# Alternating emission of two heads' scores and two quarters' state space inputs, with the causal masks behind the scores

## The chip, the cores and the metric

The kernel runs on one core of a Trainium2 chip. The metric is the time of one execution on the device in microseconds. Three runs of the kernel before stand beside one profiled execution, which has a time of its own.

## The reference, cut to what matters

Four transformer layers over 256 tokens with a width of 1024 follow each other. The change lies in the third one, whose mixer has two halves: a stick-breaking attention of eight heads of 64, and a state space model of 32 groups with 64 complex states each.

```python
def stick_breaking_attention(q, k, v):            # per block of 128 queries
    z = jnp.einsum('bqhd,bshd->bhqs', q_b, k) * scale
    causal = (spos[None, :] < tpos[:, None])[None, None]
    log_beta = jax.nn.log_sigmoid(z)
    log_1mb = jnp.where(causal, jax.nn.log_sigmoid(-z), 0.0)
    csum = jnp.cumsum(log_1mb, axis=-1)
    log_w = log_beta + csum[..., -1:] - csum
    w = jnp.where(causal, jnp.exp(log_w), 0.0)
    return jnp.einsum('bhqs,bshd->bqhd', w, v)

def s5_ssm(u, ...):
    bu_r = jnp.einsum('bsgc,gnc->bsgn', uf, bbar_r)     # the inputs
    bu_i = jnp.einsum('bsgc,gnc->bsgn', uf, bbar_i)
    x = lax.associative_scan(...)                       # x[s] = a x[s-1] + bu[s]
    return (jnp.einsum('gcn,bsgn->bsgc', c_re, x_r)     # the outputs
            - jnp.einsum('gcn,bsgn->bsgc', c_im, x_i) + d * uf)

def mixer_sb_ssm(x, ...):
    a_out = stick_breaking_attention(q, k, v)
    y = gelu(s5_ssm(u, ...))
    y = y * sigmoid(y @ w_glu + b_glu)
    return concatenate([a_out, y]) @ w_out
```

## The kernel before

All weights are read from HBM in the order of one list and split into a high part (ScalarE, L363) and a low part (VectorE, some on GpSimd, L366). A large product is then three matmuls with full 128 rows: high by high, high by low, low by high (`mm3`, L388 to L390). These products run all the time; they are called the stream here. In the third layer's mixer, while the stream computes keys, queries and values (the names sk, sq, sv in the list), two generators stand at the side and are advanced one step at each `yield` of the stream: `side_attention` and `_ssm_run`. The instructions that they emit are then ordered by the scheduler that builds the program; each engine runs its own in that order, one behind the other. The order can be read from the built program.

`side_attention` goes over the eight heads. `stage_a` writes the scores of one head into one bank of PSUM: a causal mask by a matmul of the identity (L1324, 128 rows), then keys by queries, whose 64 dimensions lie in rows 0 to 63 or 64 to 127 (L1325, and L1327 for the second block of keys). ScalarE and VectorE make the softplus of it (L1330 to L1333). `stage_b` subtracts its sums with triangular matmuls in the same bank (L1338, L1340, L1342) and takes the exponential (L1345). `stage_c` multiplies two heads by the values (L1353). Banks come from a pool of four, called psw; a head holds its bank from the scores to the exponential.

`_ssm_run` takes the 16 pairs of groups in four sets (k) of four quarters (q). A quarter's input is two matmuls of 64 rows (L1887) into a bank; the quarter's number decides which half of the rows. VectorE rotates it (L1891, L1892), GpSimd combines (L1893, L1894), VectorE scans over the tokens (L1896, two scans a quarter), and VectorE and GpSimd rotate back (L1906 to L1913). `outputs` (L1851, L1856, L1859) multiplies the states by the output matrix for the set before, and VectorE adds the skip term (L1861). The scans of a set write a buffer that the outputs of an earlier set read. Behind the last set come the gelu (ScalarE and VectorE, L1659 to L1664), its high and low parts (L464, L465) and the gate's matmuls (`glu`), which the stream's next products need. [...]

Of the kernel before, what the change touches and what calls it, by code (L numbers as in the profile page):

```python
# [11 lines left out]
AF = mybir.ActivationFunctionType  # L12
ALU = mybir.AluOpType
# [482 lines left out]
class _Norm(_Act):  # L496
# [8 lines left out]
    def slice(self, xT, c):  # L505
        self.add(xT[:, 2 * c:2 * c + 2], self.g[:, 2 * c:2 * c + 2])
        if c == 0:
            self.e.after = self.last
        self.square(xT, c)
# [779 lines left out]
def _second(e, K, xT, act, S, ln, out, dump):  # L1289
    nc, tc = e.nc, e.tc  # L1290
    V, A, G, PE = nc.vector, nc.scalar, nc.gpsimd, nc.tensor
# [3 lines left out]
    D = {}  # L1295
# [4 lines left out]
    for c in range(2):  # L1300
        e.run(e.transposed(("su", c), act,
                           lambda b, bank, c=c: A.activation(out=uT[:, 2 * c:2 * c + 2], in_=bank, func=AF.Copy)))
# [13 lines left out]
    smask2 = im[:, 1].unsqueeze(1).to_broadcast([128, 2, 128])  # L1316
    sc, ws = {}, {}

    def stage_a(s):
        j, g = s // 2, s % 2  # L1320
        hs = slice(64 * g, 64 * g + 64)
        ps = e.bank()
        diag = ps[:, :].rearrange("p (a q) -> p a q", a=4)[:, 0:4:2]
        PE.matmul(out=diag, lhsT=im[:, 0], rhs=smask2, start=True, stop=False, skip_group_check=True)  # L1324
        PE.matmul(out=ps[:, 0:256], lhsT=kT[hs, j, 0:128], rhs=qT[hs, j, :], start=False, stop=False,  # L1325
                  skip_group_check=True)
        PE.matmul(out=ps[:, 256:384], lhsT=kT[hs, j, 128:256], rhs=qT[hs, j, 128:256], start=False, stop=False,  # L1327
                  skip_group_check=True)
        l = e.t("b2", [128, 384])
        A.activation(out=l, in_=ps[:, :384], func=AF.Abs)  # L1330
        A.activation(out=l, in_=l, func=AF.Exp, scale=-1.0)
        A.activation(out=l, in_=l, func=AF.Ln, bias=1.0)
        V.scalar_tensor_tensor(out=l, in0=ps[:, :384], scalar=0.0, in1=l, op0=ALU.max, op1=ALU.add)  # L1333
        sc[s] = (ps, l)

    def stage_b(s):
        ps, sp = sc.pop(s)
# [22 lines left out]
        D["done"] = j + 1  # L1360

    def side_attention():
        ready, lag = [], 1
        for s in range(8 + lag):
            while s >= 4 and "qk" not in D:
                yield
            if s < 8:
                stage_a(s)
            if s >= lag:
                stage_b(s - lag)  # L1370
                if (s - lag) % 2:
                    ready.append((s - lag) // 2)
            yield
            if ready and "v" in D:
                stage_c(ready.pop(0))
        while ready:
            yield
            stage_c(ready.pop(0))
# [464 lines left out]
def _ssm_run(e, P, C, S, uT, yT):  # L1843
# [32 lines left out]
    for k in range(4):  # L1876
        w = e.t("b4", [128, 4, 2, 128])
        xs = e.t("b4", [128, 4, 2, 128])
        s = slice(4 * k, 4 * k + 4)
        mt = e.t("b2", [128, 4, 128])  # L1880
        G.tensor_tensor(out=mt, in0=C["j01"].unsqueeze(1).to_broadcast([128, 4, 128]),
                        in1=S["m"][:, s].unsqueeze(2).to_broadcast([128, 4, 128]), op=ALU.mult)
        for q in range(4):
            h = slice(64 * (q % 2), 64 * (q % 2) + 64)
            ps = e.bank()[:, :256].rearrange("p (c j) -> p c j", c=2)
            for c in range(2):
                PE.matmul(out=ps[:, c], lhsT=S["bT"][h, c, 2 * k + q // 2], rhs=up[h, k, q // 2])  # L1887
            st = 4 * k + q
            tc_ = e.t("b1", [128, 2, 128])
            ts_ = e.t("b1", [128, 2, 128])  # L1890
            V.tensor_tensor(out=tc_, in0=ps, in1=S["cos"][:, st].unsqueeze(1).to_broadcast([128, 2, 128]), op=ALU.mult)  # L1891
            V.tensor_tensor(out=ts_, in0=ps, in1=S["sin"][:, st].unsqueeze(1).to_broadcast([128, 2, 128]), op=ALU.mult)  # L1892
            G.tensor_tensor(out=w[:, q, 0], in0=tc_[:, 0], in1=ts_[:, 1], op=ALU.add)  # L1893
            G.tensor_tensor(out=w[:, q, 1], in0=tc_[:, 1], in1=ts_[:, 0], op=ALU.subtract)  # L1894
            for c in range(2):
                V.tensor_tensor_scan(out=xs[:, q, c], data0=mt[:, q], data1=w[:, q, c], initial=0.0,  # L1896
                                     op0=ALU.mult, op1=ALU.add)
            if q % 2:
                yield
        if prev is not None:  # L1900
            outputs(*prev)
        cosb = S["cos"][:, s]
        sinb = S["sin"][:, s]
        ta = e.t("b2", [128, 4, 128])
        tb = e.t("b2", [128, 4, 128])
        V.tensor_tensor(out=ta, in0=xs[:, :, 0], in1=cosb, op=ALU.mult)  # L1906
        G.tensor_tensor(out=tb, in0=xs[:, :, 1], in1=sinb, op=ALU.mult)
        V.tensor_tensor(out=w[:, :, 0], in0=ta, in1=tb, op=ALU.subtract)
        tc2 = e.t("b2", [128, 4, 128])
        td = e.t("b2", [128, 4, 128])  # L1910
        V.tensor_tensor(out=tc2, in0=xs[:, :, 1], in1=cosb, op=ALU.mult)
        G.tensor_tensor(out=td, in0=xs[:, :, 0], in1=sinb, op=ALU.mult)
        V.tensor_tensor(out=w[:, :, 1], in0=tc2, in1=td, op=ALU.add)  # L1913
        prev = (k, w)
        yield
# [176 lines left out]
```

## Time and profile before

| what | value |
|---|---|
| three runs | 1475.64, 1476.12, 1477.32 us, median 1476.12 |
| profiled execution | 1473.14 us, its span 1471.4 us, mean granted clock of TensorE 0.993 |
| busy share of the span | TensorE 98%, VectorE 74%, ScalarE 53%, GpSimd 19% |
| the stretch of the change | about 896 to 967 us of the span |

The span reaches from the first to the last instruction in the trace. Busy shares are averages over stages with different limits. A matmul's record is longer than the time to the next one's start, since matmuls overlap; what a matmul takes of TensorE is read from start to start.

### The profile page before, as it was taken

How to read it: one execution, taken by the hardware profiler on the slowest of the kernel's cores; microseconds unless marked ns; L12 is line 12 of the kernel's file. 1: busy time of each engine (PE TensorE's matmuls, PEld its weight loads, DVE VectorE, ACT ScalarE, POOL GpSimd, SP SyncE). 2: the span in 40 equal slices, each digit the busy share in tenths (PEclk: the TensorE clock that was granted, in tenths of full speed). 3: DMA queues.
4: the chain of work that ended last, by engine and by line, in shares of the span. 5: the costliest groups of instructions: out<-in, count | busy, mean ns of one | idle time of the engine just before them, and what ended most of it. 6: DMA issues, size and time to landing. Idle time of an engine off the chain costs nothing.

```text
span 1471.4 us, 24711 instructions
## 1 busy us (share of the span) xinstructions
PE 1435.8 (98%) x9636; PEld 1269.1 (86%) x9636; DVE 1090.3 (74%) x1820; ACT 784.9 (53%) x1258; POOL 274.5 (19%) x201
## 2 busy tenths in 40 slices
PE   9999999999999999999999999999999998999997
PEld 6878999999998779999999998778888796788886
DVE  7796669666678696679877778877666688686666
ACT  6665545444556564455645555365444465654442
POOL 2343314000045343213000337510000100100000
PEclk9999999999999999999999999999999998999999
DMA  8553555655546653555565453336556362366551
GB/s 291 188 179 109 173 172 177 198 186 187 178 146 195 198 172 130 173 166 191 188 198 180 154 185 122 101 129 216 192 181 198 123 220 75 100 208 193 186 190 69
DMA packets 70677, 250.66 MB, mean 170 GB/s; under 512 B 8096, under 2 KB 8480, under 8 KB 70560
## 3 DMA queue, kind: packets, MB, share of 16 engines
q1 hardware_dynamic: 70560, 249.07, 51.6%
q8 instruction: 76, 1.25, 0.3%
q14 instruction: 41, 0.34, 0.1%
HBM read 247.99 MB, written 1.05 MB: 169 GB/s over the span
## 4 chain that ended last, share of the span: by engine, by line
PE 49%; DVE 4%; issue 1%; ACT 1%; POOL 0%; DVEq 0%; POOLq 0%
PE psw L438 11%; PE psa L388 9%; PE psa L390 9%; PE psa L389 9%; PE psw L440 6%; DVE lo L366 1%; DVE b L1896 1%; PE psw L2033 1%; PE psw L389 0%; PE psw L2019 0%; PE psw L390 0%; ACT b L1607 0%; PE psw L1887 0%; PE psw L388 0%; DVE b L1984 0%
## 5 line engine op out<-in xcount | busy, mean ns | idle before, releaser
L366 DVE TENSOR_TENSOR lo<-raw,hi 128x1024 fp32r<-128x1024 f32 (+1 forms) x409 | 512.5, 1260 | 216.7 <-ACT hi L363 215.9
L363 ACT ACTIVATE hi<-raw 128x1024 fp32r<-128x1024 f32 (+1 forms) x448 | 465.7, 1047 | 386.8 <-issue 141.4
L438 PE MATMUL psw<-act,hi 128*128 128x512 f32 x960 | 340.7, 397 | 0.0
L440 PE MATMUL psw<-act,lo 128*128 128x256 f32 x960 | 268.0, 281 | 0.0
L438 PEld LDWEIGHTS psw<-act,hi 128*128 128x128 f32 x960 | 179.9, 188 | 41.0
L440 PEld LDWEIGHTS psw<-act,lo 128*128 128x128 f32 x960 | 181.5, 189 | 1.7
L390 PE MATMUL psa<-b,lo 128*128 128x256 f32 x640 | 180.5, 283 | 0.0
L389 PE MATMUL psa<-b,hi 128*128 128x256 f32 x640 | 180.2, 283 | 0.0
L388 PE MATMUL psa<-b,hi 128*128 128x256 f32 x640 | 177.8, 283 | 0.0
L388 PE MATMUL psa<-act,hi 128*128 128x256 f32 x456 | 132.2, 291 | 0.0
L390 PE MATMUL psa<-act,lo 128*128 128x256 f32 x456 | 130.3, 286 | 0.5 <-DVE lo L366 0.5
L389 PE MATMUL psa<-act,hi 128*128 128x256 f32 x456 | 130.8, 287 | 0.0
L366 POOL TENSOR_TENSOR lo<-raw,hi 128x1024 fp32r<-128x1024 f32 x39 | 96.0, 2461 | 173.7 <-ACT hi L363 158.9
L389 PE MATMUL psa<-lo,act 128*128 128x512 f32 (+2 forms) x320 | 121.6, 383 | 3.6 <-DVE lo L366 2.6
L388 PE MATMUL psa<-hi,act 128*128 128x512 f32 (+2 forms) x320 | 122.3, 390 | 1.6 <-ACT hi L363 1.2
L390 PEld LDWEIGHTS psa<-b,lo 128*128 128x128 f32 x640 | 122.1, 191 | 0.1
L389 PEld LDWEIGHTS psa<-b,hi 128*128 128x128 f32 x640 | 122.0, 191 | 0.0
L388 PEld LDWEIGHTS psa<-b,hi 128*128 128x128 f32 x640 | 120.5, 191 | 1.2
L390 PE MATMUL psa<-hi,act 128*128 128x512 f32 (+2 forms) x320 | 117.9, 382 | 0.0
L388 PE MATMUL psa<-hi,b 128*128 128x512 f32 x256 | 99.7, 391 | 0.0
L389 PE MATMUL psa<-lo,b 128*128 128x512 f32 x256 | 99.6, 390 | 0.0
L390 PE MATMUL psa<-hi,b 128*128 128x512 f32 x256 | 98.7, 389 | 0.0
(360 smaller groups left out, 2692.2 us busy)
## 6 DMA issues: line engine op xcount, KB each, us to landing
raw<-in_ws_dram SPq DMA_DIRECT2D x450, 512.0 KB, 4.1
b<-in_ln_dram SPq DMA_DIRECT2D x8, 512.0 KB, 5.1
raw<-in_ws_dram SPq DMA_DIRECT2D x8, 280.0 KB, 3.7
raw<-in_ws_dram SPq DMA_DIRECT2D x4, 264.0 KB, 2.7
b<-in_x_dram SPq DMA_DIRECT2D x4, 256.0 KB, 5.0
out_dram<-b SPq DMA_DIRECT2D x4, 256.0 KB, 2.0
cb<-in_cb_dram SPq DMA_DIRECT2D x1, 676.0 KB, 7.1
b<-in_p_dram SPq DMA_DIRECT2D x2, 256.0 KB, 5.0
```

The costliest lines, as they stand in the source:

```text
L363: self.nc.scalar.activation(out=hi, in_=w, func=AF.Copy)
L366: eng.tensor_tensor(out=lo, in0=w, in1=hi.bitcast(F32), op=ALU.subtract)
L388: mm(out=out, lhsT=lh, rhs=rh, start=start, stop=False, skip_group_check=shared)
L389: mm(out=out, lhsT=lh, rhs=rl, start=False, stop=False, skip_group_check=shared)
L390: self.mlast = mm(out=out, lhsT=ll, rhs=rh, start=False, stop=stop, skip_group_check=shared)
L438: mm(out=bank.rearrange("p (v t) -> p v t", v=2), lhsT=h[:, c], rhs=act[2][k], start=k == 0, stop=False, skip_group_check=True)
L440: mm(out=bank[:, :256], lhsT=l[:, c], rhs=act[0][k], start=False, stop=k == len(hi) - 1, skip_group_check=True)
L1896: V.tensor_tensor_scan(out=xs[:, q, c], data0=mt[:, q], data1=w[:, q, c], initial=0.0, op0=ALU.mult, op1=ALU.add)
L2033: PE.matmul(out=o[64 * gg:64 * gg + 64, q0:256], lhsT=vw[:, kt, v0:v0 + 64], rhs=pts[s - 1 + gg][:, 256 * kt:256 * kt + 256 - q0], start=k ...
```

## The change

`stage_a` now handles a pair of heads j: it takes two banks, emits the first score matmul of both heads, then the second of both, and the two masks behind them. The softplus of both heads follows. `side_attention` goes over four pairs and runs `stage_b` of both heads a step later. In `_ssm_run` the inputs of two quarters are emitted together, alternating between the halves of the rows, into two banks. What is computed stays the same.

```diff
@@ -1316,22 +1316,26 @@
     smask2 = im[:, 1].unsqueeze(1).to_broadcast([128, 2, 128])
     sc, ws = {}, {}
 
-    def stage_a(s):
-        j, g = s // 2, s % 2
-        hs = slice(64 * g, 64 * g + 64)
-        ps = e.bank()
-        diag = ps[:, :].rearrange("p (a q) -> p a q", a=4)[:, 0:4:2]
-        PE.matmul(out=diag, lhsT=im[:, 0], rhs=smask2, start=True, stop=False, skip_group_check=True)
-        PE.matmul(out=ps[:, 0:256], lhsT=kT[hs, j, 0:128], rhs=qT[hs, j, :], start=False, stop=False,
-                  skip_group_check=True)
-        PE.matmul(out=ps[:, 256:384], lhsT=kT[hs, j, 128:256], rhs=qT[hs, j, 128:256], start=False, stop=False,
-                  skip_group_check=True)
-        l = e.t("b2", [128, 384])
-        A.activation(out=l, in_=ps[:, :384], func=AF.Abs)
-        A.activation(out=l, in_=l, func=AF.Exp, scale=-1.0)
-        A.activation(out=l, in_=l, func=AF.Ln, bias=1.0)
-        V.scalar_tensor_tensor(out=l, in0=ps[:, :384], scalar=0.0, in1=l, op0=ALU.max, op1=ALU.add)
-        sc[s] = (ps, l)
+    def stage_a(j):
+
+        pss = [e.bank() for _ in range(2)]
+        for o, n in ((0, 128), (256, 256)):
+            for g in range(2):
+                hs = slice(64 * g, 64 * g + 64)
+                PE.matmul(out=pss[g][:, o:o + 384 - n],
+                          lhsT=kT[hs, j, n - 128:n], rhs=qT[hs, j, n - 128:256], start=o == 0, stop=False,
+                          skip_group_check=True)
+        for g in range(2):
+            diag = pss[g].rearrange("p (a q) -> p a q", a=4)[:, 0:4:2]
+            PE.matmul(out=diag, lhsT=im[:, 0], rhs=smask2, start=False, stop=False, skip_group_check=True)
+        for g in range(2):
+            ps = pss[g]
+            l = e.t("b2", [128, 384])
+            A.activation(out=l, in_=ps[:, :384], func=AF.Abs)
+            A.activation(out=l, in_=l, func=AF.Exp, scale=-1.0)
+            A.activation(out=l, in_=l, func=AF.Ln, bias=1.0)
+            V.scalar_tensor_tensor(out=l, in0=ps[:, :384], scalar=0.0, in1=l, op0=ALU.max, op1=ALU.add)
+            sc[2 * j + g] = (ps, l)
 
     def stage_b(s):
         ps, sp = sc.pop(s)
@@ -1360,19 +1364,18 @@
         D["done"] = j + 1
 
     def side_attention():
-        ready, lag = [], 1
-        for s in range(8 + lag):
-            while s >= 4 and "qk" not in D:
+        ready = []
+        for j in range(4):
+            while j >= 2 and "qk" not in D:
                 yield
-            if s < 8:
-                stage_a(s)
-            if s >= lag:
-                stage_b(s - lag)
-                if (s - lag) % 2:
-                    ready.append((s - lag) // 2)
+            stage_a(j)
             yield
-            if ready and "v" in D:
-                stage_c(ready.pop(0))
+            for g in range(2):
+                stage_b(2 * j + g)
+                if ready and "v" in D:
+                    stage_c(ready.pop(0))
+            ready.append(j)
+            yield
         while ready:
             yield
             stage_c(ready.pop(0))
@@ -1881,10 +1884,13 @@
         G.tensor_tensor(out=mt, in0=C["j01"].unsqueeze(1).to_broadcast([128, 4, 128]),
                         in1=S["m"][:, s].unsqueeze(2).to_broadcast([128, 4, 128]), op=ALU.mult)
         for q in range(4):
-            h = slice(64 * (q % 2), 64 * (q % 2) + 64)
-            ps = e.bank()[:, :256].rearrange("p (c j) -> p c j", c=2)
-            for c in range(2):
-                PE.matmul(out=ps[:, c], lhsT=S["bT"][h, c, 2 * k + q // 2], rhs=up[h, k, q // 2])
+            if q % 2 == 0:
+                pss = [e.bank()[:, :256].rearrange("p (c j) -> p c j", c=2) for _ in range(2)]
+                for c in range(2):
+                    for n in range(2):
+                        h = slice(64 * n, 64 * n + 64)
+                        PE.matmul(out=pss[n][:, c], lhsT=S["bT"][h, c, 2 * k + q // 2], rhs=up[h, k, q // 2])
+            ps = pss[q % 2]
             st = 4 * k + q
             tc_ = e.t("b1", [128, 2, 128])
             ts_ = e.t("b1", [128, 2, 128])
```

Below, three places of the two orders. The line numbers of the changed kernel are a few higher: the scores are its L1325, the mask L1330, the last step of the softplus L1337, the triangular matmuls L1342, L1344 and L1346, the inputs of a quarter L1892, GpSimd's part L1899 and L1900, the scans L1902, the last rotation L1919 and the outputs L1854, L1859 and L1862. The order names a scan SCALAR_TENSOR_TENSOR.

TensorE, where the inputs of k = 1 begin, before (psw is a bank; the number behind it tells banks apart):

```order
L1887 MATMUL psw_10231<-b_1691_10035,b_1487_8648 128x128 x2
L1887 MATMUL psw_10242<-b_1691_10035,b_1487_8648 128x128 x2
L1324 MATMUL psw_10253<-b_1683_9995 128x2x128
L1325 MATMUL psw_10253<-b_1680_9992,b_1681_9993 128x256
L1327 MATMUL psw_10253<-b_1680_9992,b_1681_9993 128x128
```

and now:

```order
L1892 MATMUL psw_10231<-b_1691_10035,b_1487_8648 128x128
L1892 MATMUL psw_10232<-b_1691_10035,b_1487_8648 128x128
L1892 MATMUL psw_10231<-b_1691_10035,b_1487_8648 128x128
L1892 MATMUL psw_10232<-b_1691_10035,b_1487_8648 128x128
L1325 MATMUL psw_10253<-b_1680_9992,b_1681_9993 128x256
L1325 MATMUL psw_10254<-b_1680_9992,b_1681_9993 128x256
L1325 MATMUL psw_10253<-b_1680_9992,b_1681_9993 128x128
L1325 MATMUL psw_10254<-b_1680_9992,b_1681_9993 128x128
L1330 MATMUL psw_10253<-b_1683_9995 128x2x128
L1330 MATMUL psw_10254<-b_1683_9995 128x2x128
```

The two quarters alternate, head 1 (psw_10254) has come up from 24 stream matmuls farther down to stand beside head 0, and the masks are last. Heads 6 and 7 stand in the same way later; head 3 stands 14 stream matmuls behind head 2, head 5 nine behind head 4.

TensorE, at the outputs of k = 0 (psw_10365) and the triangular matmuls of heads 0 and 1 (psw_10253, psw_10254), now:

```order
L1854 MATMUL psw_10365<-b_1664_9866,b_1512_8803 128x128
L1859 MATMUL psw_10365<-b_1692_10069,b_1455_8452 32x128 x4
L1325 MATMUL psw_10394<-b_1680_9992,b_1681_9993 128x256
L1325 MATMUL psw_10394<-b_1680_9992,b_1681_9993 128x128
L1859 MATMUL psw_10365<-b_1692_10069,b_1455_8452 32x128 x4
L1862 MATMUL psw_10365<-b_1692_10069,b_1455_8452 32x127 x6
L1342 MATMUL psw_10253<-b_1736_10261,cb_7507 128x256
L1344 MATMUL psw_10253<-b_1736_10261,ones_64 128x128
L1346 MATMUL psw_10253<-b_1736_10261,cb_7507 128x128
L1342 MATMUL psw_10254<-b_1737_10266,cb_7507 128x256
```

Before, head 0's triangular matmuls stood in the middle of these outputs and head 1's behind them; both are now in one row near the end, behind the scores of head 2 (psw_10394). 26 stream matmuls stand between this place and the second set of quarters ahead of it, where there were 24.

VectorE at the same place, before (b_1735 and b_1743 are the softplus of heads 0 and 1):

```order
L1913 TENSOR_TENSOR b_1692_10069<-b_1716_10185,b_1717_10186 128x4x128
L1333 SCALAR_TENSOR_TENSOR b_1735_10257<-psw_10253,b_1735_10257 128x384
L1896 SCALAR_TENSOR_TENSOR b_1726_10228<-b_1727_10229,b_1725_10227 128x128 x4
L1333 SCALAR_TENSOR_TENSOR b_1743_10313<-psw_10309,b_1743_10313 128x384
L366 TENSOR_TENSOR lo_10475<-raw_10106,hi_10474 128x1024
```

and now:

```order
L1919 TENSOR_TENSOR b_1692_10069<-b_1716_10185,b_1717_10186 128x4x128
L1902 SCALAR_TENSOR_TENSOR b_1726_10228<-b_1727_10229,b_1725_10227 128x128 x4
L1337 SCALAR_TENSOR_TENSOR b_1736_10261<-psw_10253,b_1736_10261 128x384
L1902 SCALAR_TENSOR_TENSOR b_1726_10228<-b_1727_10229,b_1725_10227 128x128
L1337 SCALAR_TENSOR_TENSOR b_1737_10266<-psw_10254,b_1737_10266 128x384
L1902 SCALAR_TENSOR_TENSOR b_1726_10228<-b_1727_10229,b_1725_10227 128x128
L366 TENSOR_TENSOR lo_10480<-raw_10106,hi_10479 128x1024
```

Four scans that stood behind head 0's softplus stand ahead of it. On GpSimd L1893 and L1894 of one quarter have moved ahead of a weight split L366 there. The order of the DMA queue is unchanged. In the fourth layer's sparse attention, which the change doesn't touch, the scheduler has moved a few value products (L2033) and score matmuls past each other.

## Rows read from the trace of the kernel before

**Rows 1.** The page, busy us of an engine, share, instructions.

```profile
PE 1435.8 (98%) x9636; PEld 1269.1 (86%) x9636; DVE 1090.3 (74%) x1820; ACT 784.9 (53%) x1258; POOL 274.5 (19%) x201
```

**Rows 2.** Windows: stretch, length, busy PE, PEld, DVE, ACT, POOL, clock, DMA, GB/s.

```profile
912.00:919.00 7.00, 5.99 (x46) 5.26 (x45) 7.00 (x12) 3.52 (x7) 4.78 (x3) 1.00 0.25 77
```

**Rows 3.** Waits of PE from 896 to 968: us in total, times, longest.

```profile
PE psw L1338 <- DVE b L1333: 2.2, 3, 1.0
```

**Rows 4.** Timeline of DVE: scans of k = 2, and the way out.

```profile
928.54 4.72 DVE L1896 TENSOR_TENSOR_SCAN b<-b,b 128x128 f32<-128x128 f32 x8 [2.06 <-PE psw L1859]
...
952.71 0.68 DVE L1913 TENSOR_TENSOR b<-b,b 128x512 f32<-128x512 f32 x1
...
955.39 0.48 DVE L1861 SCALAR_TENSOR_TENSOR b<-b,prm,psw 128x256 f32<-128x256 f32 x1 [1.68 <-PE psw L1859]
...
964.30 1.23 DVE L465 TENSOR_TENSOR b<-b,b 128x1024 fp32r<-128x1024 f32 x1
```

**Rows 5.** Timeline of PE: outputs of k = 3, and the gate's first matmuls.

```profile
954.25 0.65 PE L1856 MATMUL psw<-b,b 128*32 128x128 f32 x16
...
966.96 0.39 PE L390 MATMUL psa<-hi,act 128*128 128x512 f32 x1
967.19 0.41 PE L388 MATMUL psw<-b,hi 128*128 128x256 f32 x2
```

**Rows 6.** Timeline of PE around one quarter: start, us, instruction.

```profile
886.01 0.71 PE L1887 MATMUL psw<-b,b 64*128 64x128 f32 x4
886.65 0.39 PE L388 MATMUL psa<-act,hi 128*128 128x256 f32 x1
```

**Rows 7.** Timeline of PE, two quarters and one head's scores.

```profile
900.71 0.28 PE L389 MATMUL psa<-act,hi 128*128 128x256 f32 x1
900.83 0.28 PE L390 MATMUL psa<-act,lo 128*128 128x256 f32 x1
901.04 0.72 PE L1887 MATMUL psw<-b,b 64*128 64x128 f32 x8
901.69 0.38 PE L1324 MATMUL psw<-b 128*128 128x256 f32 x1
902.00 0.70 PE L1325 MATMUL psw<-b,b 64*128 64x256 f32 x2
...
902.85 0.39 PE L388 MATMUL psa<-act,hi 128*128 128x256 f32 x1
```

**Rows 8.** Timeline of DVE at the outputs of k = 0.

```profile
905.39 0.86 DVE L1913 TENSOR_TENSOR b<-b,b 128x512 f32<-128x512 f32 x1
906.18 0.54 DVE L1333 SCALAR_TENSOR_TENSOR b<-psw,b 128x384 f32<-128x384 f32 x1
906.64 3.71 DVE L1896 TENSOR_TENSOR_SCAN b<-b,b 128x128 f32<-128x128 f32 x4
...
911.87 1.36 DVE L1896 TENSOR_TENSOR_SCAN b<-b,b 128x128 f32<-128x128 f32 x4
```

**Rows 9.** Timeline of POOL at the same place.

```profile
905.67 2.81 POOL L366 TENSOR_TENSOR lo<-raw,hi 128x1024 fp32r<-128x1024 f32 x1
```

**Rows 10.** Timeline of PE, end of the outputs of k = 0 (idle before, releaser).

```profile
910.87 0.70 PE L1338 MATMUL psw<-b,cb 128*128 128x256 f32 x2 [0.74 <-DVE b L1333]
...
911.76 0.36 PE L388 MATMUL psa<-act,hi 128*128 128x256 f32 x1
```

**Rows 11.** A long wait of PE in the timeline.

```profile
1172.48 0.41 PE L1599 MATMUL psw<-ca,b 128*128 128x128 f32 x2 [2.65 <-DVE b L1562]
```

**Rows 12.** The window behind that wait, columns as in the other window.

```profile
1174.40:1177.90 3.50, 3.50 (x19) 3.50 (x18) 2.99 (x8) 3.50 (x7) 0.00 (x0) 0.51 0.00 0
```

**Rows 13.** Timeline of PE, value products of the sparse attention, whole and split.

```profile
1264.70 0.87 PE L2033 MATMUL psw<-b,b 128*64 128x256 f32 x8
...
1268.48 0.65 PE L2033 MATMUL psw<-b,b 128*64 128x256 f32 x2
...
1269.42 0.86 PE L2033 MATMUL psw<-b,b 128*64 128x256 f32 x6
```

## The prediction

> **What bounds the kernel now.** The page's busy times say TensorE, 1435.8 us of a span of 1471.4 [rows 1], so at first sight each matmul saved is time saved. I looked at the stretch that the change touches, 896 to 968 us, by its windows, then laid the timelines of TensorE, VectorE and GpSimd side by side. From 912 to 919 us VectorE is busy for 7.00 of 7.00 us and TensorE for 5.99 [rows 2]: here VectorE, which runs the state space scans, ends last. The list of TensorE's waits names one line, L1338, three times, 2.2 us in all, for L1333, VectorE's last step of the softplus [rows 3]. The stage leaves through one chain: the last rotation of quarter set k = 3 (L1913) ends at 953.39, TensorE gets to the outputs of k = 3 (L1856) at 954.25, VectorE adds the skip term (L1861) at 955.39, the gelu ends with the low halves (L465) at 965.53, and the gate's matmuls need them [rows 4]. They start at 967.19 [rows 5]. So the chain has 0.87 us of slack ahead of L1856 and 1.66 behind L465. What counts is when the gate's matmuls start; from there on the order is the same up to the sparse attention.
>
> **The change, step by step.**
>
> Prices on TensorE. One quarter alone takes 0.64 us from its start to the next instruction's, two quarters that follow each other 0.65 (901.04 to 901.69) [rows 6, 7]. So two halves of the rows already run side by side when they stand together, emitted alternately or not: for quarters the change saves only where it brings separated ones together. A head's scores take 1.16 us (901.69 to 902.85): mask 0.31, the four records of its scores 0.85 [rows 7]. Of this some 0.2 is lost at each change between full and half rows: the last stream matmul before a half-row block starts 0.21 ahead of its follower where 0.12 is usual (900.71, 900.83, 901.04), and the mask, one pass of 256 columns, takes 0.31. Two heads that stand together should take what one takes, some 0.65 for the four half-row matmuls, and with two masks behind them about 0.9 instead of 2.3. That saves 1.4.
>
> How many pairs. The order shows two of four, heads 0 and 1, and heads 6 and 7. Heads 2, 3 and heads 4, 5 stand 14 and 9 stream matmuls apart. They save 0.1 a pair, a switch less. One set of quarters beside heads 6 and 7 also comes together, another 0.6. TensorE's work falls by 1.4 + 0.1 + 0.1 + 1.4 + 0.6 = 3.6 us. A rule of the Trainium skill speaks against the change: row tiles write to different banks and so press on PSUM (TensorEngine Tiling, section Restrictions and Gotchas). The order agrees, since head 3 takes its bank only behind head 0's exponential; by that rule the saving stays at two pairs, and by the twofold speed of the same page's section Theoretical Speedup it would be 5.6 us for four.
>
> What the order does with it. At the outputs of k = 0, VectorE had L1333 of head 0 straight behind L1913, at 906.18, then four scans, 3.71 us, then head 1's [rows 8]. Now the four scans stand ahead of both. On GpSimd one quarter's L1893 and L1894 now stand ahead of the weight split L366, which ran from 905.67 to 908.48 [rows 9]; four scans beside it took 3.71 us, four others 1.36 [rows 8], so it falls on the scans again, about 1 us later. VectorE ends L1913 near 906.3, the scans near 910.3, head 0's softplus near 910.8 (911.5 if the split delays two scans in turn). TensorE gets to head 0's L1338 (now L1342) near 907.4: 902.85 [rows 7], less the 1.4 saved, with 26 stream matmuls at 0.12, makes 904.6 for the block's start; outputs in two parts take some 1.7 (1.1 from 954.25 to L1861's 955.39 [rows 4, 5], the first matmul 0.3, and two switches less the last two matmuls), head 2's scores 1.1. So it stands idle for 3.4 us, from 907.4 to 910.8. Then come two heads of about 0.9, two output matmuls and a mask, 0.3 each: the stream resumes at 913.2 to 913.6, where it now does at 911.76 [rows 10]. Behind L1342 wait all of TensorE's stream, head 3's scores and the next quarters. The saving of heads 0 and 1 is spent, and 1.4 more (913.4 less 911.76, less 0.24 for the two matmuls done).
>
> The next gate. The old waits of L1338 behind this place, the longest with 1.0 and one of 0.4 (2.2 less 1.0 less the 0.74 of 910.87 [rows 3, 10]), go, since its successors stand farther behind their softplus. But the outputs of k = 1, which the eight scans of k = 2 wait for (they idle 2.06 us and start at 928.54 [rows 4]), now have heads 3, 4 and 5 and a longer piece of the stream ahead of them. From 913.4: 22 narrow stream matmuls 2.7, three single heads at 1.06 3.2, two pairs of quarters with their switches 1.7, two L1342 groups at 0.9 (910.87 to 911.76 [rows 10]) 1.8, 31 wide stream matmuls at 0.23 (966.96 to 967.19 [rows 5]) 7.1, outputs 1.3. That is 17.8, so the scans start near 931.3, 2.8 later. They then run clear of GpSimd's next split, which now overlaps the first of them, and should take 2.8 us, at the pace of the undisturbed four [rows 8], 0.34 each, instead of 4.72 [rows 4], which gives 1.9 back. One more L465 (0.35) now stands ahead of the last L1913. VectorE, busy to the end, so ends it at 953.4 + 2.8 - 1.9 + 0.35 = 954.7.
>
> The way out. TensorE, in the same way, waits near 945 for the softplus of heads 6 and 7, then has three value products and 13 wide stream matmuls (3 now) ahead of the outputs of k = 3; I put it there at 956.0. The outputs end at 957.0 and the gelu chain, 10.1 us from L1861's start to the end of L465 [rows 4], loses 0.3 because no other L465 stands in it: the gate's matmuls start near 966.9, where they now start at 967.19. That is a gain of 0.3. Bounds: -2.5 (both slacks used up) and +2.5 (another 2.5 us of late scans).
>
> The clock. The idle 3.4 us at 907.4 is longer than the wait of 2.65 us at 1169.8, after which the granted clock stood at 0.51 from 1174.40 to 1177.90, that is at 1.2 GHz [rows 11, 12]. Half of 3.4 us is 1.7 us of TensorE time, and the outputs of k = 1 are on its way. It may not come, or be hidden where VectorE ends last anyway: between 0 and 1.7, I take half, 0.9.
>
> The sparse attention. At two places, some 270 us later, a group of L2033 is split by other matmuls. Whole it takes 0.87 us, in two parts 0.65 and 0.86 [rows 13]: up to 0.6 each where TensorE ends last, nothing where the softmax does. Between 0 and 1.2; I take 0.5, since which of the two ends last there changes from step to step. DMAs: the order of SP's queue is the same; nothing to add.
>
> **Sum.** -0.3 + 0.9 + 0.5 = +1.1 us. The profiled execution took 1473.14 us (span 1471.4 and 1.7 around it); the median of the three runs is 1476.12, the same kernel 0.2% higher. The change goes on either: 1477.2 for the median. A measurement of this kernel can tell about 0.2% (3 us) from no change.
>
> **The rivals.**
>
> A: TensorE's time comes through. If VectorE interleaves better than I laid out (scans without delay, softplus by 909), TensorE waits little at 907.4, k = 1 comes on time, and what is saved stays: 3.6 and the old waits of 1.4, less 0.5 for the sparse attention, and the rest of the chain's slack spent: 4.1 to 4.5 us, about 1471.8. For it: TensorE's 98% [rows 1]. Against it: VectorE's full window [rows 2] and its own instructions, which are as many as before. It decides if the scans of k = 2 start before 928.5. Chance 0.15. The Trainium skill's twofold speed (TensorEngine Tiling, Theoretical Speedup) points this way; the trace bears it out for two quarters [rows 6, 7], and the order for two pairs of heads of four.
>
> B: the waits turn into a slow clock twice. TensorE idles at 907.4 and again near 945, each is followed by a stretch at 1.2 GHz, and both push the scans: -0.3 + 2 x 1.7 + 0.9 = +4.0, about 1480.1. For it: the one wait over 2.6 us [rows 11, 12]. Against it: the second wait is cut up by other work. It decides if two such stretches appear in 905 to 960. Chance 0.19.
>
> C: the heads do not run side by side, so that the change doesn't do what it says: +1.3 for two pairs on TensorE, of which the wait at 907.4 hides the first: +0.7 on my sum, 1477.9. The equal times of one quarter and two [rows 6, 7] speak against it. Chance 0.05; it falls within 0.2%.
>
> **How the numbers follow.** My forecast has 0.61 and C 0.05, both inside 0.2%: same 0.66, A is the faster 0.15, B the slower 0.19. The forecast's own range goes from -2.0 to +3.0 (bounds of the way out, clock and attention, not all at once): 1474.1 to 1479.1. To leave out no more than 2 in 10 it reaches to about A and B: 1472.6 to 1480.4.
>
> **What would show it.** Right: records of heads 0 and 1 in pairs and 0.9 us for both; a wait of 3 us or more at L1342 for L1337 between 907 and 912; scans of k = 2 starting near 931; the gate's matmuls within 2 us of 967.2; a wait of TensorE ahead of them for the gelu. Wrong: a wait under 1.5 us at L1342; scans before 928.5; the stage's end moved by over 3 us either way; or a difference that arises after 1000 us.

## The result, and the profile after

The changed kernel takes 1484.12 us (median of 18 runs, 1476.29 to 1488.25); the kernel before, on the same chip, 1475.62 us (18 runs). The ratio is 1.0053, 95% interval 1.0043 to 1.0064: slower by about 8.5 us, 0.5%, and outside the predicted range. The profiled execution took 1483.53 us at a mean granted clock of 0.987, where before it was 1473.14 us at 0.993. The time of the 18 runs goes with the granted clock: the one at 0.993 took 1476.29 us, the one at 0.983 took 1488.25.

The page of the changed kernel shows the same number of matmuls, busy for 2.7 us more instead of 3.6 us less [rows 1]:

```profile
PE 1438.5 (97%) x9636; PEld 1273.2 (86%) x9636; DVE 1088.4 (73%) x1820; ACT 785.2 (53%) x1258; POOL 271.8 (18%) x201
```

I compare one stage in all kernels: from the first input matmul of the state space to ScalarE's first tanh of the gate. It holds 605 records of matmuls in both kernels. Before, it reached from 886.01 [rows 6] to 970.39, that is 84.38 us, with TensorE busy for 82.20 at clock 1.00 (columns as in [rows 2]):

```profile
886.01:970.39 84.38, 82.20 (x605) 66.68 (x605) 72.53 (x112) 39.97 (x62) 45.00 (x46) 1.00 0.30 98
```

The windows of the changed kernel give the whole stage first, then three pieces of it:

```profile
889.22:979.54 90.32, 82.35 (x605) 68.41 (x605) 70.93 (x112) 39.54 (x62) 42.91 (x46) 0.94 0.30 99
...
911.30:914.50 3.20, 0.00 (x0) 0.00 (x0) 3.20 (x5) 0.00 (x0) 2.46 (x3) 0.77 0.19 61
914.50:919.80 5.30, 5.25 (x20) 4.28 (x21) 4.31 (x9) 1.28 (x3) 2.35 (x2) 0.50 0.48 163
...
948.50:954.00 5.50, 3.77 (x18) 3.57 (x19) 5.50 (x13) 1.31 (x4) 2.51 (x6) 0.69 0.70 229
```

The stage is 5.94 us longer. TensorE does nothing from 911.3 to 914.5, and then runs at 0.50, that is at 1.2 GHz; this is called half clock below. The granted clock was down from 913.01 to 919.84 and again from 950.56 to 953.97, 10.2 us in all; before, it was 1.00 throughout the stage. Of the other 4.4 us, 3.2 arose ahead of the stage (it starts at 889.22 for 886.01), where this execution ran at half clock from 848.16 to 854.98, and 1.2 behind it. The half clock at 848 follows an idle of 1.97 us that the kernel before has too, with 2.00 us, and there none followed; so these 3.2 us need not come from the change.

The waits of TensorE from 890 to 980 (total, times, longest) are five, where the list from 896 to 968 before had L1338 alone, with 2.2 us [rows 3]:

```profile
PE psw L1342 <- DVE b L1337: 3.3, 1, 3.3
PE psw L1892 <- DVE b L1898: 1.8, 1, 1.8
PE psw L388 <- ACT b L464: 1.3, 1, 1.3
PE psw L1854 <- DVE b L1898: 0.9, 1, 0.9
PE psw L389 <- DVE b L465: 0.8, 1, 0.8
```

TensorE's timeline shows heads 0 and 1 as a pair (each score matmul stands as two records, so eight for both), the two idles in brackets, the outputs of k = 3, and the gate's first matmuls [rows 5, 7, 10]:

```profile
899.37 0.72 PE L1892 MATMUL psw<-b,b 64*128 64x128 f32 x8
899.92 0.82 PE L1325 MATMUL psw<-b,b 64*128 64x256 f32 x8
900.67 0.50 PE L1330 MATMUL psw<-b 128*128 128x256 f32 x2
901.01 0.28 PE L388 MATMUL psa<-act,hi 128*128 128x256 f32 x1
...
914.54 1.22 PE L1342 MATMUL psw<-b,cb 128*128 128x256 f32 x2 [3.25 <-DVE b L1337]
...
919.20 0.42 PE L390 MATMUL psa<-act,lo 128*128 128x256 f32 x1
...
950.23 0.89 PE L1892 MATMUL psw<-b,b 64*128 64x128 f32 x4 [1.76 <-DVE b L1898]
...
964.64 0.64 PE L1859 MATMUL psw<-b,b 128*32 128x128 f32 x16
...
975.23 0.51 PE L388 MATMUL psw<-b,hi 128*128 128x256 f32 x2 [1.34 <-ACT b L464]
976.49 0.39 PE L389 MATMUL psw<-b,hi 128*128 128x256 f32 x1 [0.76 <-DVE b L465]
```

VectorE's timeline at the same places [rows 4, 8] has the four scans ahead of both softplus, then the scans of k = 2, and the way out:

```profile
909.28 0.68 DVE L1919 TENSOR_TENSOR b<-b,b 128x512 f32<-128x512 f32 x1
909.88 4.16 DVE L1902 TENSOR_TENSOR_SCAN b<-b,b 128x128 f32<-128x128 f32 x4
913.96 0.53 DVE L1337 SCALAR_TENSOR_TENSOR b<-psw,b 128x384 f32<-128x384 f32 x1
...
937.66 2.63 DVE L1902 TENSOR_TENSOR_SCAN b<-b,b 128x128 f32<-128x128 f32 x8 [1.75 <-PE psw L1862]
...
965.79 0.48 DVE L1864 SCALAR_TENSOR_TENSOR b<-b,prm,psw 128x256 f32<-128x256 f32 x1 [1.09 <-PE psw L1862]
...
975.21 1.23 DVE L465 TENSOR_TENSOR b<-b,b 128x1024 fp32r<-128x1024 f32 x1
```

GpSimd's weight split falls on these four scans, as before on others [rows 9]:

```profile
910.24 2.46 POOL L366 TENSOR_TENSOR lo<-raw,hi 128x1024 fp32r<-128x1024 f32 x1
```

And ScalarE's timeline in the gelu shows two weight splits (L363) between its two steps, where one stood before. The line of that one comes first, then the changed kernel. There the second split waits 1.01 us for the stream, and the table load and the tanh stand behind it:

```profile
958.20 1.06 ACT L363 ACTIVATE hi<-raw 128x1024 fp32r<-128x1024 f32 x1 [0.90 <-PE psa L390]
```

```profile
967.33 1.05 ACT L363 ACTIVATE hi<-raw 128x1024 fp32r<-128x1024 f32 x1
969.39 1.06 ACT L363 ACTIVATE hi<-raw 128x1024 fp32r<-128x1024 f32 x1 [1.01 <-PE psa L390]
970.47 1.28 ACT L1665 ACT_TABLE_LOAD   x1
971.77 1.06 ACT L1665 ACTIVATE b<-b 128x1024 f32<-128x1024 f32 x1
```

Behind the stage, in the sparse attention of the fourth layer, the last six records of the value products stand 302.01 us behind the stage's end before and 303.31 us behind it now:

```profile
1272.40 0.86 PE L2033 MATMUL psw<-b,b 128*64 128x256 f32 x6
```

```profile
1282.85 0.86 PE L2039 MATMUL psw<-b,b 128*64 128x256 f32 x6
```

### The profile page after: what moved, and what is told of

The parts are those of the page before. It is cut to its first block, busy times and chain, and to the rows that moved or that the text cites. A ratio compares the mean times of both kernels' runs of the same rounds, so it can differ in the third digit from the quotient of the medians.

```text
span 1481.8 us, 24709 instructions
## 1 busy us (share of the span) xinstructions
PE 1438.5 (97%) x9636; PEld 1273.2 (86%) x9636; DVE 1088.4 (73%) x1820; ACT 785.2 (53%) x1258; POOL 271.8 (18%) x201
## 4 chain that ended last, share of the span: by engine, by line
PE 48%; DVE 5%; issue 2%; ACT 1%; POOL 0%; DVEq 0%; POOLq 0%
PE psw L438 11%; PE psa L388 9%; PE psa L390 8%; PE psa L389 8%; PE psw L440 6%; DVE lo L366 1%; PE psw L2039 1%; DVE b L1902 1%; DVE b L1990 0%; PE psw L389 0%; PE psw L2025 0%; PE psw L390 0%; ACT b L1610 0%; DVE b L1963 0%; PE psw L388 0%
## 5 line engine op out<-in xcount | busy, mean ns | idle before, releaser
L366 DVE TENSOR_TENSOR lo<-raw,hi 128x1024 fp32r<-128x1024 f32 (+1 forms) x409 | 512.9, 1261 | 218.9 <-ACT hi L363 218.2
L363 ACT ACTIVATE hi<-raw 128x1024 fp32r<-128x1024 f32 (+1 forms) x448 | 466.1, 1047 | 386.9 <-issue 141.6
L388 PE MATMUL psa<-act,hi 128*128 128x256 f32 x456 | 134.0, 295 | 0.0
L389 PE MATMUL psa<-act,hi 128*128 128x256 f32 x456 | 132.5, 291 | 0.0
L366 POOL TENSOR_TENSOR lo<-raw,hi 128x1024 fp32r<-128x1024 f32 x39 | 96.0, 2462 | 176.3 <-ACT hi L363 170.3
```

Of the source, the lines that this page charges most:

```text
L363: self.nc.scalar.activation(out=hi, in_=w, func=AF.Copy)
L366: eng.tensor_tensor(out=lo, in0=w, in1=hi.bitcast(F32), op=ALU.subtract)
L388: mm(out=out, lhsT=lh, rhs=rh, start=start, stop=False, skip_group_check=shared)
L389: mm(out=out, lhsT=lh, rhs=rl, start=False, stop=False, skip_group_check=shared)
```

## The experiments

Theory 1: the loss is mostly the half clock that follows TensorE's idles, and goes with the idles. Theory 2: VectorE's late order costs what it costs at any clock. Theory 3: alternation gains nothing, and waits only move. In the experiments that move or add single instructions, every other instruction keeps the place that it had in the kernel it starts from; edits are then shown as the order of an engine. The stage times of all are in one table:

| kernel | ratio to before, 95% | stage, us | PE busy | clock | longest idles of TensorE, us |
|---|---|---|---|---|---|
| before | | 84.38 | 82.20 | 1.00 | 1.0, 0.7 |
| changed | 1.0053 (1.0043 to 1.0064) | 90.32 | 82.35 | 0.94 | 3.3, 1.8, 1.3, 0.9, 0.8 |
| changed again | 1.0039 (1.0025 to 1.0054) | 90.35 | 82.38 | 0.94 | 3.3, 1.8, 1.3, 0.9, 0.8 |
| only quarters | 0.9993 (0.998 to 1.0005) | 84.60 | 82.07 | 1.00 | 1.2, 1.0 |
| only scores | 1.0056 (1.0034 to 1.0078) | 90.09 | 83.88 | 0.95 | 2.6, 1.8, 1.1, 0.8 |
| masks first | 1.0053 (1.004 to 1.0066) | 93.34 | 87.52 | 0.95 | 2.8, 1.8, 0.6 |
| idles filled | 1.0026 (1.0015 to 1.0037) | 86.44 | 83.10 | 1.00 | 1.3, 0.9, 0.8 |
| late softplus in before | 1.0032 (1.0019 to 1.0045) | 88.61 | 85.20 | 0.96 | 3.0 |
| softplus first | 1.0016 (1.0006 to 1.0027) | 87.48 | 81.81 | 0.96 | 1.8, 1.3, 1.0 |
| softplus first, last quarter later | 1.003 (1.0015 to 1.0045) | 87.28 | 81.86 | 0.96 | 1.5, 1.3, 0.9 |
| gate early | 1.0039 (1.0024 to 1.0053) | 87.80 | 79.77 | 0.98 | 3.3, 1.8, 1.3 |
| these three moves | 1.0017 (1.0005 to 1.0029) | 86.97 | 81.56 | 0.96 | 1.5, 1.3, 0.9 |
| splits behind | 1.0027 (1.0015 to 1.0038) | 87.37 | 81.22 | 0.96 | 3.2, 1.8, 0.8 |
| all idles moved away | 0.9983 (0.9973 to 0.9994) | 80.96 | 77.97 | 1.00 | 1.1, 1.0, 0.9 |

The stage is that of one profiled execution; the ratio is over all runs. TensorE's busy time with the idles filled holds 4.8 us of the filler.

**The two parts alone.** Each keeps one part of the change.

```diff
 only quarters: _ssm_run as changed, stage_a and side_attention as before
 only scores:   stage_a and side_attention as changed, _ssm_run as before
```

> Only the state space inputs of two quarters are alternated; the scores are emitted head by head as before, and the softplus of the first head stands ahead of the scans as before. Theories 1 and 2: no new idle over 2 us on TensorE at the first outputs, no fall of the clock, and the small saving of alternated quarters (about 0.5 us a set, mostly beside other work): 1474.5 to 1476.5 us. Theory 3: half of the loss, 1478 to 1481 us.

> Only the scores of two heads are alternated, with the masks behind; the state space inputs are emitted as before. The scheduler puts the first head's softplus ahead of the scans of the second set and the second head's behind five of them, so the wait now stands at L1342 of the second head. Theory 1: an idle of about 3 us there, half clock behind it, 1480 to 1484 us. Theory 2: the idle alone, less the 2 us that alternation saves on TensorE: 1476.5 to 1478 us.

The quarters alone took 1474.25 us (before 1475.47): no measurable difference, with the clock at 1.00 and only the old waits. The scores alone took 1482.43 us, inside theory 1's range: the whole loss. The idle stands at the second head, as the order says (2.58 us at 910.17), and half clock from 910.42 to 913.83 goes with it; the gate waits too (1.8 and 0.8 us), and had half clock behind it as well (968.44, 6.83 us). So the loss comes with the scores.

**Idles filled.** Work that nothing reads keeps TensorE busy in both idles; what is listed with a matmul m stands directly behind it.

```diff
+    def fill(bank, n):
+        ones = e.ones.bitcast(BF16)
+        return [PE.matmul(out=bank[:, 256:512], lhsT=ones[:, :128], rhs=ones, start=False, stop=False,
+                          skip_group_check=True) for _ in range(n)]
...
-                    PE.matmul(out=y[h, 0, 1:128], lhsT=S["cexp"][:, v, 4 * k + q], rhs=w[:, q, c, 0:127],
+                    m = PE.matmul(out=y[h, 0, 1:128], lhsT=S["cexp"][:, v, 4 * k + q], rhs=w[:, q, c, 0:127],
...
+                if (k, v, q) == (0, 3, 1):
+                    _EXTRA.append((m, fill(b, 27)))
...
+                        if (k, q, c, n) == (3, 2, 1, 0):
+                            _EXTRA.append((m, fill(bs[0], 14)))
```

> The changed kernel in its own order, with bf16 matmuls on constants of 256 columns each put into the two places where TensorE idles: 27 of them ahead of L1342 of the first head (idle of 3.25 us) and 14 ahead of the last quarter's input (idle of 1.8 us). They write columns of PSUM that nothing reads; no other instruction moves. Theory 1, the half clock behind the two idles is the loss that the prediction undersized: the granted clock stays at its upper level in this stretch, L1342 still waits for VectorE to the same moment, and the 10.2 us at half clock (913.0 to 919.8, 950.6 to 954.0) go; each gives back half of itself, so about 5 us: 1478 to 1480.5 us. Theory 2, the loss is VectorE's late order and would be there at any clock: no gain, 1483 to 1485.5 us.

It took 1479.44 us (before 1475.47), inside theory 1's range, 4.7 less than the changed kernel in its first set of runs and 2.4 less than in its second. The filler (L1853) stands where the idle was; L1342 still waits for VectorE, and starts 25.33 us after the stage's start as in the changed kernel (914.95 less 889.62, and 914.54 less 889.22: 25.32):

```profile
911.62 3.12 PE L1853 MATMUL psw<-ones 128*128 128x256 bf16 x27
914.95 0.70 PE L1342 MATMUL psw<-b,cb 128*128 128x256 f32 x2 [0.21 <-DVE b L1337]
```

The windows show 1.00 where the changed kernel had 0.50 and 0.69, and the whole stage last:

```profile
914.50:919.80 5.30, 5.09 (x37) 4.24 (x35) 5.30 (x10) 2.52 (x5) 1.95 (x2) 1.00 0.52 170
948.00:954.00 6.00, 5.82 (x64) 4.89 (x64) 6.00 (x16) 0.49 (x1) 3.03 (x7) 1.00 0.56 178
...
889.62:976.06 86.44, 83.10 (x646) 68.92 (x646) 71.98 (x112) 39.51 (x62) 43.65 (x46) 1.00 0.32 106
```

The scans of k = 2, the outputs of k = 3, and the way from their skip term to the low halves (here L1913, L1865, L1872 and L465):

```profile
935.63 2.63 DVE L1913 TENSOR_TENSOR_SCAN b<-b,b 128x128 f32<-128x128 f32 x8 [1.76 <-PE psw L1868]
...
961.16 0.65 PE L1865 MATMUL psw<-b,b 128*32 128x128 f32 x16
...
962.30 0.48 DVE L1872 SCALAR_TENSOR_TENSOR b<-b,prm,psw 128x256 f32<-128x256 f32 x1 [1.10 <-PE psw L1868]
...
971.72 1.22 DVE L465 TENSOR_TENSOR b<-b,b 128x1024 fp32r<-128x1024 f32 x1
```

With every real wait in its place, the stage is 3.9 us shorter (90.32 to 86.44). That is the clock's share in these two profiles, and near theory 1's 5; theory 2 expected nothing. The granted clock of all runs agrees: on the mean it is 0.992 in the 84 runs of the kernel before that have one on record, 0.987 and 0.989 in the two sets of the changed kernel, and 0.991 here. The 2.06 us that remain against 84.38 are what the waits at full clock cost beyond what the pairing saves.

**The wait in the kernel before.** VectorE's order there, one row moved.

```diff
 L1913 TENSOR_TENSOR
-L1333 SCALAR_TENSOR_TENSOR    (softplus of head 0)
 L1896 TENSOR_TENSOR_SCAN x4
+L1333 SCALAR_TENSOR_TENSOR
 L1333 SCALAR_TENSOR_TENSOR    (softplus of head 1)
```

> The kernel before in its own order, but the softplus (L1333) of head 0 stands behind the four scans of the second set instead of ahead of them; nothing of the change is in it. TensorE then idles about 2.6 us at the first head's L1338 (from 907.8 to about 910.45), and its later wait of 1.0 us for the second head is overlapped, so the stream resumes about 1.5 us later. Theory 1 (an idle of this length at this place brings half clock behind it): half clock for 3.4 to 6.8 us directly behind, 1.7 to 3.4 us more: 1478.7 to 1480.5 us, against 1475.5 of before. Theory 2 (only the order of VectorE costs): 1476.5 to 1477.5 us and no half clock there.

It took 1480.2 us (before 1474.25 in this set), inside theory 1's range, without any of the change. TensorE's timeline and the window behind the idle:

```profile
911.79 0.70 PE L1338 MATMUL psw<-b,cb 128*128 128x256 f32 x2 [2.98 <-DVE b L1333]
```

```profile
912.80:919.60 6.80, 6.80 (x41) 5.86 (x40) 6.80 (x11) 2.40 (x5) 4.78 (x3) 0.50 0.24 80
```

The stage grows by 4.23 us; if the idle itself has the 1.5 expected of it, the rest, 2.7, goes to the 6.83 us at half clock. So one late instruction on VectorE costs over half of what the whole change does.

**Softplus first**, in the changed kernel, then with a second move, on VectorE and TensorE:

```diff
 L1919 TENSOR_TENSOR
+L1337 SCALAR_TENSOR_TENSOR x2
 L1902 TENSOR_TENSOR_SCAN x4
-L1337 SCALAR_TENSOR_TENSOR    (and the second, a scan later)
second run also:
 L1892 MATMUL (k=3, q=2)
-L1892 MATMUL (k=3, q=3)
 L1413 MATMUL x8
+L1892 MATMUL (k=3, q=3)
```

> The changed kernel in its own order, but the softplus (L1337) of heads 0 and 1 stands ahead of the four scans (L1902) that it waits behind, right behind L1919 of the first set; nothing else moves. Theories 1 and 2 both say that the idle of 3.25 us at L1342 goes. Theory 1: the half clock that followed it goes too (6.8 us at half clock, worth 3.4), while the second idle (1.8 us) and its 1.7 stay: 1477 to 1479.5 us. Theory 2: the idle alone comes back, less the 1 us by which the scans are now later: 1481 to 1482.5 us. Theory 3, the alternation itself is what costs, and waits only move: 1483.5 to 1485 us.

> The changed kernel in its own order with two moves: the softplus of heads 0 and 1 ahead of the four scans, and the input matmuls of the last quarter (which wait 1.8 us for a bank of PSUM) behind the eight residual matmuls (L1413) that follow them. Theory 1: no idle over 1.5 us is left between 905 and 960, the half clock near 943 that the run with the first move alone still had goes as well (1.8 us of idle and up to 3.4 us of clock): 1473 to 1475.5 us. Theory 2: only the idle of 1.8 us comes back: 1475.5 to 1476.5 us. Theory 3, waits only move: 1477 to 1478 us as with the first move alone.

The first took 1477.42 us, inside theory 1's range; the idle of 3.25 us and its half clock are gone, the second idle (1.77 us) now brought 6.83 us of half clock from 943.61. The second move failed: 1478.88 us (before 1474.25), over the ranges of all three theories. The idle went from the quarter to the next instruction that needs a bank, and half clock followed again (TensorE's timeline, and the window):

```profile
943.63 0.46 PE L1854 MATMUL psw<-b,b 128*128 128x128 f32 x2 [1.52 <-DVE b L1898]
```

```profile
944.40:947.80 3.40, 3.40 (x34) 2.52 (x22) 2.36 (x6) 0.15 (x1) 1.09 (x4) 0.50 0.18 60
```

Here theory 3 was nearest, and right that the wait only moved: the cause is VectorE, which comes late to L1898, not the place of the quarter.

**The gate early**, alone and with both moves above.

```diff
TensorE:
+L1859, L1862 MATMUL (outputs of k=3)
 L1357 MATMUL x4 (heads 6 and 7)
 L388, L389, L388 MATMUL
-L1859, L1862 MATMUL
VectorE: L1864 ahead of the last L465; ScalarE: L1662 ahead of the last L464
```

> The changed kernel in its own order with the way to the gate shortened alone: the outputs of the last set (L1859, L1862) stand ahead of the values of heads 6 and 7 (L1357) on TensorE, and their skip term (L1864) and the first ScalarE step of the gelu (L1662) each ahead of the last split of the attention's output (L465, L464). The idles at L1342 and at the last quarter stay, with their half clock. The waits of the gate's matmuls (1.34 and 0.76 us) shrink by about 1.9 together: 1482 to 1483 us. Rival: the gate's matmuls have to wait for something else, and the time stays: 1483.5 to 1485 us.

> The changed kernel with all the moves: softplus of heads 0 and 1 ahead of the scans, the last quarter's input behind the residual's matmuls, the last outputs ahead of the values of heads 6 and 7 with their skip term and gelu. Nothing else moves. Theory 1: without idles no half clock in this stage, and the 3.6 us that alternation saves on TensorE show in the time: 1471 to 1473.5 us, faster than before. Theory 3, alternation gains nothing and waits only move: 1475.5 to 1477.5 us.

The first took 1480.63 us (before 1474.25), under both ranges; its profile has no half clock behind the last quarter's idle of 1.77 us, which both had counted on. The gate's waits did not shrink: 1.34 and 0.76 us as before the move. My theory of the way out fell, and what the rival said of the waits held. ScalarE's timeline shows why: the gelu starts earlier, but the second split now waits 1.65 us instead of 1.01 for the stream, so the table load starts at the same place of the stream.

```profile
963.25 1.06 ACT L363 ACTIVATE hi<-raw 128x1024 fp32r<-128x1024 f32 x1 [1.65 <-PE psa L390]
```

The run with all three moves took 1476.36 us (before 1474.25), short of the 1471 to 1473.5 expected and inside theory 3's 1475.5 to 1477.5: the idle at L1854 and the gate's waits were still there, each with a half-clock stretch behind it (944.50 and 968.40, 3.41 us each).

**Splits behind, masks first, and all idles moved away**, on the same chip with the changed kernel again.

```diff
splits behind, ScalarE (VectorE's L366 likewise):
 L363 ACTIVATE
-L363 ACTIVATE
 L1665 ACT_TABLE_LOAD, ACTIVATE
+L363 ACTIVATE
-L363 ACTIVATE
 L464 ACTIVATE
+L363 ACTIVATE
masks first: in stage_a, before the scores, with start=True
all idles: softplus first, gate early, splits behind, and on VectorE
-L366 TENSOR_TENSOR
 L1897, L1898 TENSOR_TENSOR (k=3, q=1)
+L366 TENSOR_TENSOR
```

> The changed kernel once more, unaltered, so that the three others can be compared with it on the same chip. All theories: 1482.5 to 1485.5 us, with half clock behind the idle at L1342 and, in part of the executions, behind the idle at the last quarter's input.

> The changed kernel in its own order, but on ScalarE the weight split (L363) that stands between the two steps of the gelu and waits for the stream comes behind the second step (L1665), and the split after it behind the gelu's high part (L464); their low parts on VectorE (L366) move likewise. The earlier run that brought the gelu's begin forward left the gate's waits at 1.3 and 0.8 us; if the split is what holds the gelu, these waits (2.1 us together) go here: 1480.5 to 1482.5 us. If the gelu is held by something else, or the later splits make the stream wait afterwards: 1483 to 1485.5 us.

> The changed kernel with the masks ahead of the scores again (L1330 before L1325), in the order that the scheduler then makes; on VectorE the softplus of heads 0 and 1 still stands behind the four scans. Theory 1 and 2: the place of the masks costs and saves nothing that shows, the idle at L1342 stays: 1482 to 1486 us. Rival, the masks behind the scores hold up the softplus and so the wait: 1478 to 1481 us.

> The changed kernel in its own order with the idles removed by moves alone: the softplus of heads 0 and 1 ahead of the four scans; VectorE's weight split (L366, 2.05 us) that stood ahead of the rotation of the third quarter (k=3, q=1) behind it, so that its bank comes free about 2 us earlier; the last set's outputs with their skip term and the gelu's first step ahead of the last values; the two weight splits out of the gelu. Theory 1: no idle of TensorE over 1.4 us between 905 and the gate, no half clock in the stage, the 3.6 us that alternation saves are seen: 1468.5 to 1472 us, faster than before. Theory 3, alternation gains nothing and waits only move: 1474 to 1477 us.

The changed kernel took 1481.89 us here (before 1475.46), a little under its expectation. With the splits behind it took 1480.11, just under its range: the gate's wait for L464 is gone from the list of waits and that for L465 is 0.3 us, so the split was what held the gelu.

```profile
PE psw L389 <- DVE b L465: 0.3, 1, 0.3
```

Masks first took 1483.28, as expected by theories 1 and 2, but something else changed that I had not seen: in TensorE's timeline the second mask now stands between the two heads' matmuls, and two of the eight records run by themselves.

```profile
900.32 0.38 PE L1324 MATMUL psw<-b 128*128 128x256 f32 x1
900.63 0.70 PE L1328 MATMUL psw<-b,b 64*128 64x256 f32 x2
901.26 0.38 PE L1324 MATMUL psw<-b 128*128 128x256 f32 x1
901.57 0.92 PE L1328 MATMUL psw<-b,b 64*128 64x256 f32 x6
```

The pair takes 2.10 us (900.32 to 902.42) instead of 1.09 (899.92 to 901.01). In this order the masks behind the scores are what keeps the two heads side by side.

With all idles moved away the kernel took 1473.78 us against 1475.46, ratio 0.9983 (0.9973 to 0.9994), and is faster than the kernel before, by 0.2%, and than the changed one. That is above the 1468.5 to 1472 expected of theory 1 and just under the 1474 to 1477 of theory 3. The whole stage in one window:

```profile
889.99:970.95 80.96, 77.97 (x605) 65.18 (x605) 70.74 (x112) 39.53 (x62) 44.43 (x46) 1.00 0.32 106
```

No half clock is in it, and the stage is 3.42 us shorter than before, which speaks for theory 1. Of this 1.7 us are seen in the medians. The sparse attention takes most of the rest: its last value products stand 304.02 us behind the stage's end (1274.97 less 970.95), 2.0 later than before. The same moves without the pairing were not run, so the runs don't show how much of the 1.7 us is the pairing's and how much the moves'.

## Why the prediction was wrong

**What was right.** The prices on TensorE: heads 0 and 1 take 1.09 us where 0.9 was put. In the kernel without idles TensorE is busy for 77.97 us in the stage instead of 82.20, so the 3.6 us that the change takes off TensorE are there, or a little more. The order's effect at the outputs of k = 0: an idle of 3.25 us at L1342 for L1337 (3.4 predicted), with the scans ahead of both softplus and GpSimd's split upon them. The scans of k = 2 ran in 2.63 us (2.8 predicted). A wait ahead of the gate for the gelu was there too. The rule of the Trainium skill that row tiles press on PSUM (TensorEngine Tiling, section Restrictions and Gotchas) agrees with the trace: heads 6 and 7 hold two of the four banks, and the last quarter waits 1.76 us until L1898 has read the quarter in another.

**The step that failed** is the clock: "It may not come, or be hidden where VectorE ends last anyway: between 0 and 1.7, I take half, 0.9." It came twice and was not hidden. In both profiles of the changed kernel the granted clock was at its lower level for 10.2 us of the stage, behind the idle at L1342 for 6.83 us, twice what I had taken, and behind the idle for a bank for 3.41. The filled idles measure its share as 3.9 us. Less the 3.21 us by which the stage starts later, the scans of k = 2 start at 934.45 where I had 931.3, 3.1 late. With the idles filled they start 46.01 us into the stage instead of 48.44 (935.63 less 889.62, 937.66 less 889.22). So 2.4 us of the first slow stretch, of which TensorE worked for 5.3 us, went through the scans to the end, and 1.5 us came from the second. The sign that I had named, the stage's end moved by over 3 us, is there with 5.94. Rival B had this mechanism, the place of the second idle within 2 us, and 1480.1 us; it took one stretch of 3.4 us at each place, gave the second idle to the softplus instead of a bank, and has 0.9 us in its sum for which the prediction gives no source.

**A second term was mis-sized**: the way out. I had the gate's matmuls 0.3 us earlier. At full clock, with the idles filled, the stage is 2.06 us longer than before. The outputs of k = 3 start 71.54 us into it (961.16 less 889.62) where I had 69.99 (956.0 less 886.01). The gelu chain behind them takes 10.64 us (962.30 to 972.94) where I had 9.8, its old length less 0.3: two weight splits now stand inside it on ScalarE where one stood, and the second waits for the stream. With the second behind the tanh (splits behind) 2.1 us of waits fall to 0.3. Those +2.06 lie near the upper bound that I gave this term.

**A third term was mis-sized**: the sparse attention, put at 0.5, at most 1.2. The order behind the stage is the same in the kernel before and in late softplus, and in both the last six records of the value products stand 302.01 us behind the stage's end. In the five kernels that have the changed kernel's order there and as much half clock on this way (13.65 us) they stand at 303.27 to 304.02, so the new order costs 1.3 to 2.0 us. Which of the moved instructions costs it was not tested.

**The sum** with the measured terms is +3.9 for the clock, +2.1 for the way out and +1.3 to 2.0 for the sparse attention, +7.3 to 8.0 us, where I had +1.1. The medians rose by 8.5 us in the first set of runs and by 6.4 in the second. The runs don't show whether half clock ahead of the stage, which other kernels had near 850 too, comes more often with the change.

**The rivals.** A did not come by itself; with four other moves the last experiment has 1.7 us of the 4.3 that it promised. C is excluded by the timeline of heads 0 and 1.

## What to carry to other kernels

Where TensorE is nearly full, price a new idle of it not by its own length alone: look at the granted clock in the window behind idles of that size, in more than one profile, and carry that time along the chain to the stage's end instead of halving it. When two matmul blocks are drawn together, list for each engine what now stands ahead of the instruction that frees their result or their bank; here one softplus behind four scans cost more than the pairing gained. A chain that hands the stage over, as the gelu here, should have no other work of its engine in it that waits for the stream.

## What the runs showed of the hardware

An idle of 1.52 us was followed by half clock here (3.41 us at 0.50, in the run with the last quarter later). I had looked only at the one wait of 2.65 us [rows 11, 12], and in one profile. The length alone does not decide it. In the 14 profiles that wait is followed by half clock in ten and by none in four, softplus first among them:

```profile
1176.65 0.41 PE L1602 MATMUL psw<-ca,b 128*128 128x128 f32 x2 [2.65 <-DVE b L1565]
```

```profile
1176.60:1180.00 3.40, 2.87 (x21) 2.48 (x21) 2.49 (x7) 2.37 (x7) 1.21 (x2) 1.00 0.00 0
```

The idle of 2.6 to 3.3 us at heads 0 and 1 was followed by half clock in all seven profiles that have it, the idle of 1.5 to 1.8 us for a bank in six of seven, and an idle of 1.7 us near 443 us, which all 14 have, in none. Idles up to 1.06 us in the last experiment were followed by none. The gate's two, 1.34 and 0.76 us, were followed by it with all three moves (968.40, 3.41 us) and not in the profile of the changed kernel. Behind an idle of one and the same length at one place, the slow stretch was 3.41 us in one profile and 6.83 in another (L1342, 3.25 us: 3.41 with the gate early, 6.83 in the changed kernel). With constant bf16 matmuls in that idle, 27 in 3.12 us, the clock stayed at 1.00.
